# Second head's tiles in the input's even blocks, late gates by single column blocks, front inputs over attention's keys

## The chip, the cores and the metric

The kernel runs on one core of a Trainium2 chip. TensorE (PE in the profile) multiplies matrices into PSUM; VectorE (DVE), ScalarE (ACT) and GpSimd (POOL) work on SBUF and PSUM; SyncE (SP) issues the DMAs, from one queue and in order. The metric is the time of one execution on the device in microseconds. Before the change it is 1268.46 us, the median of three runs (1268.2 to 1274.1).

## The reference

One layer of a sequence mixer for a sequence of 2048 rows of 1024 numbers, in float32. The rows are normalised and multiplied by one wide input matrix, whose columns feed two groups of heads. Their outputs are gated, concatenated, projected and added to the input:

```python
h = rms_norm(x, norm_w[l])
proj = h @ w_in[l].astype(h.dtype)
(dn_q, dn_k, dn_v, dn_z, dn_beta, dn_decay,
 sw_q, sw_k, sw_v, sw_z) = jnp.split(proj, cuts, axis=-1)
dn = gated_deltanet_bidir(dn_q, dn_k, dn_v, dn_beta, dn_decay, ...)
dn = rms_norm(dn, dn_out_norm_w[l]).reshape(b, s, DN_WIDTH)
dn = dn * jax.nn.silu(dn_z.astype(jnp.float32))
sw = windowed_gqa_with_sinks(sw_q, sw_k, sw_v, swa_q_norm_w[l], swa_k_norm_w[l], swa_sinks[l])
sw = sw * jax.nn.silu(sw_z.astype(jnp.float32))
x = x + jnp.concatenate([dn, sw], axis=-1) @ w_out[l]
```

The first group ("dn") has four heads of 128. Its q, k and v pass through a short convolution over time; then each head runs a gated delta rule in both directions. In chunks, that rule needs the products of keys inside a chunk, the inverse of a unit triangular matrix for each chunk, and then a scan over the chunks that carries a 128 x 128 state. The second group ("sw") is attention in a window of 128 rows to either side, eight query heads on two key heads.

## The kernel before

The sequence is cut into 16 chunks of 128 rows, and for the input projection into four blocks of 512 (block 0 to 3). To reach float32 accuracy on the fast matmul type each operand is split into a high and a low part (`xhi`, `xlo`; `whi`, `wlo`), and a product is three matmuls: high by high, high by low, low by high. `proj_feat` (L189) makes one such unit: 8 row groups x 3 = 24 matmuls of 128 x 512 into one PSUM bank `pf_z` or `pf_c`.

`phase_a` (L71) works in two halves of two blocks each. It prepares the blocks (`xprep_rows`, `xprep`), projects attention's q, k, v (`seq_chunk`), and then runs attention chunk by chunk (`kv_chunk`, `q_chunk`, `attend`) with other projections between: the convolved dn columns (`conv_pair`) and the gates (`gate_pairs`, L210: tanh on ScalarE and one VectorE step make the SiLU of a gate, which is stored to DRAM in `zsw_d` and `zdn_d`). The split input lies in a pool `xp` with two buffers for each part, so blocks 0 and 2 share one and blocks 1 and 3 the other. Weights are loaded by `load_w` (L175) in pairs of 128-column groups: 256 KB pieces land in a staging tile `wst`, ScalarE copies the high part and VectorE subtracts to get the low one. Attention's keys and values lie in `k2` and `v2`.

The gates of the second half are the late gates: `phase_a` returns them as a list of functions (L414), and `phase_b` (L523) runs them behind the first head's front (L862 to L864). They use the pools `xp`, `wp` and a small output pool `zp`.

For each head h, `phase_b` has four steps; the first three of one head overlap with the scan of the head before:

- `pre_front(h)` (L610), the front: in four pieces of four chunks it loads `kq` and `vt` and the decays (`gm`), transposes, forms the key products `gh` (L667) and writes them, decayed, to the tiles `ma` (L676); it also writes `ks` and `vs` and stores part of `ma` to DRAM (`m_d`).
- `solve(h)` (L698) loads that back and inverts the 32 x 32 diagonal blocks in 31 serial steps on VectorE (`tm`, L714, and L718), then stores to `x_d`.
- `invert(h)` (L721) builds the 128 x 128 inverses from them, with matmuls `pi` (L745), in four parts.
- `scan(h)` (L771) has 16 steps for each direction; each forms `pk`, `py` and `po`. Each step's matmuls wait for the state of the step before.

The tiles `ma`, `ks` and `vs` of even heads lie in the pool `hd0`, those of odd heads in `hd1`; head 2 reuses the parts of `hd0` that scan 0 has left, head 3 those of `hd1`. `hd1` is allocated on the right side of SBUF after `wide.close()` (L871), where `xp`, `wp` and `zp` lay. So are `rp` (the scan's tiles), the scan's PSUM, `kx`, and `swp`, for the output product of the attention half (`sw_units`, matmuls `pcs`), which fills gaps between heads. `out_pair` (L928) makes the last product (`pcd`). `hd0`, `q1` (the front's inputs), `qa` and `qb` lie on the left, over the tiles of phase A that attention uses.

The order of the instructions on each engine comes from a planner, `set_order` (L1009). It builds a graph of all dependencies, buffers and pools, gives every instruction a cost, and schedules forward and backward in turn (L1308 to L1315); of the last passes it keeps the best and writes its order down for all five engines, the DMA queue on SyncE included. A pool laid over closed ones is planned behind all users of those. The first pass takes instructions by the length of the path behind them (`rank`).

Of the kernel before, what the change touches and what calls it, by code (L numbers as in the profile page):

```python
# [7 lines left out]
F32 = mybir.dt.float32  # L8
# [16 lines left out]
NDEC = 1  # L25
WSB = 7
# [9 lines left out]
def tile_hybrid(ctx, tc, t, out, dbg=None):  # L36
    nc = tc.nc
    V, A, G, T = nc.vector, nc.scalar, nc.gpsimd, nc.tensor
    dma = nc.sync.dma_start

    cp = ctx.enter_context(tc.tile_pool(reuse_waits="tile", name="cp", bufs=1))
    gp = ctx.enter_context(tc.tile_pool(reuse_waits="tile", name="gp", bufs=1))
    hp = ctx.enter_context(tc.tile_pool(reuse_waits="tile", name="hp", bufs=2))
    dp = ctx.enter_context(tc.tile_pool(reuse_waits="tile", name="dp", bufs=1, space=DRAM))

    def const(name, shape, src=None, dt=F32):
        a = cp.tile(shape, dt, tag=name, name=name)
# [12 lines left out]

    mix_dn = dp.tile([4, P, S], F32, tag="mix_dn", name="mix_dn")

    with ExitStack() as cb, ExitStack() as wide:
        with ExitStack() as ca:
            consts, late = phase_a(ca, wide, tc, t, ident, nw, bd, gp, mix_sw, kq_d, v_d, zdn_d, zsw_d, dp)
        phase_b(cb, wide, late, tc, t, ident, consts, hp, mix_dn, mix_sw, kq_d, v_d, zdn_d, zsw_d, dp, out)
    if dbg is not None:
        dbg(tc, locals())


def phase_a(ctx, wide, tc, t, ident, nw, bd, gp, mix_sw, kq_d, v_d, zdn_d, zsw_d, q_pool):  # L71
# [38 lines left out]
    def xprep_rows(b, then):  # L110
        xr = bp.tile([P, 1030], F32, tag="big", name=f"xr{b}_0")
        dma(xr[:, :D], t["x"][4 * b * P : (4 * b + 1) * P, :])
        for e in (b, b + 1):
            xhi[e] = xp.tile([P, KC, 512], F32R, tag="xhi", name=f"xhi{e}")
            xlo[e] = xp.tile([P, KC, 512], F32R, tag="xlo", name=f"xlo{e}")
# [37 lines left out]
    def xprep(b):  # L153
# [6 lines left out]
        if b not in xhi:  # L160
            xhi[b] = xp.tile([P, KC, 512], F32R, tag="xhi", name=f"xhi{b}")
            xlo[b] = xp.tile([P, KC, 512], F32R, tag="xlo", name=f"xlo{b}")
# [61 lines left out]

    def conv_pair(i0, half):
# [30 lines left out]
    k2 = ap.tile([P, 2, 2, 6 * P], F32R, tag="k2", name="k2")  # L256
    v2 = ap.tile([P, 6, 2, P], F32R, tag="v2", name="v2")
# [131 lines left out]
    for half in range(2):  # L389
# [22 lines left out]
        if half:  # L412
            fill = conv
            late = sw + [lambda zp, i=i: gate_pairs([(12 + i, zdn_d[i : i + 2])], half, None, zp) for i in (0, 2)]  # L414
# [108 lines left out]
def phase_b(ctx, wide, late, tc, t, ident, consts, hp, mix_dn, mix_sw, kq_d, v_d, zdn_d, zsw_d, dp, out):  # L523
# [66 lines left out]
    q1 = pool("q1")  # L590
    qa = pool("qa", stack=pre_stack)
# [10 lines left out]
    def ma_tile(h, p):  # L602
        tag = f"ma{FREED[p] if h > 1 else p}"
        return hd[h % 2].tile([P, 4, 4, P], F32, tag=tag, name=f"ma{h}_{p}", bufs=1)

    def kv_tile(kind, h, n, name):
        p, slot = ((0, n), (1, n), (2, n) if n < 2 else (0, n - 2), (0, 2 + n) if n < 2 else (1, n - 2))[h]
        return (hd[p] if p < 2 else kx).tile([P, 4, P], F32, tag=f"{kind}{slot}", name=name, bufs=1)

    def pre_front(h):  # L610
# [12 lines left out]
        for n, c4 in enumerate(FRONT):  # L623
            s4 = slice(4 * c4, 4 * c4 + 4)
            cs = slice(c4 * 512, (c4 + 1) * 512)
            kq = q1.tile([P, 2, 512], F32, tag="kq", name=f"kq{h}_{c4}", bufs=2)
            dma(kq, kq_d[h][:, :, cs])
            vt = q1.tile([P, 512], F32, tag="vt", name=f"vt{h}_{c4}", bufs=2)
            dma(vt, v_d[h][:, cs])
            gms = []  # L630
            for d in range(2):
                gm = q1.tile([P, 4, P], F32, tag="gm", name=f"dc{h}_{c4}_{d}", bufs=4)
# [253 lines left out]
    pair = [P, 2, 512]  # L886
# [10 lines left out]
    w = [spare(q1, pair, "kq", f"wod4_{x}", 2) for x in range(2)]  # L897
    wh.append([w[0][:, k] for k in range(2)])
    wl.append([w[1][:, k] for k in range(2)])
    w = [spare(q1, flat, "gm", f"wod5_{x}", 4) for x in range(4)]  # L900
    wh.append(w[:2])
    wl.append(w[2:])
    wh.append([spare(q1, flat, "vt", f"wod6_{k}", 2) for k in range(2)])
# [105 lines left out]
def set_order(tc):  # L1009
# [298 lines left out]
    now, best = plan([-r for r in rank], True), None  # L1308
# [71 lines left out]
```

## Time and profile before

| | us |
|---|---|
| median of 3 runs | 1268.46 |
| the profiled execution | 1270.95 |
| its span, first to last instruction | 1268.8 |
| TensorE busy | 1213.9 |
| VectorE busy | 918.6 |
| ScalarE busy | 716.8 |
| GpSimd busy | 562.6 |
| DMA moved | 205.34 MB, 162 GB/s mean |

Engines overlap, so the busy times don't add up. The record of a matmul covers its whole way through the array while the next one has already begun; two records that start 0.23 us apart last 0.4 us each, so the busy share of TensorE says where it has nothing to do rather than how much it does. Instructions bear the number of a line of the kernel and the names of the tiles: `pf_z<-xhi,wh_z` is a matmul of a gate. A float32 product that isn't split leaves two records for each matmul of the program.

### The profile page before, as it was taken

How to read it: one execution, taken by the hardware profiler on the slowest of the kernel's cores; microseconds unless marked ns; L12 is line 12 of the kernel's file. 1: busy time of each engine (PE TensorE's matmuls, PEld its weight loads, DVE VectorE, ACT ScalarE, POOL GpSimd, SP SyncE). 2: the span in 40 equal slices, each digit the busy share in tenths (PEclk: the TensorE clock that was granted, in tenths of full speed). 3: DMA queues.
4: the chain of work that ended last, by engine and by line, in shares of the span. 5: the costliest groups of instructions: out<-in, count | busy, mean ns of one | idle time of the engine just before them, and what ended most of it. 6: DMA issues, size and time to landing. Idle time of an engine off the chain costs nothing.

```text
span 1268.8 us, 22319 instructions
## 1 busy us (share of the span) xinstructions
PE 1213.9 (96%) x7018; PEld 1036.2 (82%) x7018; DVE 918.6 (72%) x2200; ACT 716.8 (56%) x2143; POOL 562.6 (44%) x941
## 2 busy tenths in 40 slices
PE   6999999999999999999999999899799899999998
PEld 5998888788879998778788787788588689889777
DVE  4412388999966479999996583679569869758765
ACT  6322254766644577776755424848566955686521
POOL 1430034667622288675321305513483373582442
PEclk9999999999999999999999999999899999999999
DMA  8442344332445434432128826976964885754786
GB/s 263 142 135 67 112 150 128 119 106 76 147 148 166 129 91 113 152 98 71 59 93 253 224 71 183 280 203 193 270 189 154 260 209 152 227 175 142 239 275 207
DMA packets 225765, 205.34 MB, mean 162 GB/s; under 512 B 48752, under 2 KB 175344, under 8 KB 225648
## 3 DMA queue, kind: packets, MB, share of 16 engines
q1 hardware_dynamic: 225648, 203.92, 53.0%
q8 instruction: 56, 0.92, 0.3%
q14 instruction: 61, 0.50, 0.1%
HBM read 138.79 MB, written 65.08 MB: 161 GB/s over the span
## 4 chain that ended last, share of the span: by engine, by line
PE 66%; DVE 11%; DMA 9%; ACT 8%; POOL 2%; issue 2%; SPq 1%; DVEq 0%; ACTq 0%; POOLq 0%
PE pf_c L194 4%; PE pf_c L195 4%; PE pf_c L196 4%; PE pf_z L194 4%; PE pf_z L195 4%; PE pf_z L196 4%; PE pi L745 3%; DVE acc L245 3%; PE pt L366 3%; DMA xr<-x 3%; PE pq_q L205 2%; PE pq_q L207 2%; PE pq_q L206 2%; PE pcd L958 2%; PE pcd L960 2%
## 5 line engine op out<-in xcount | busy, mean ns | idle before, releaser
L194 PE MATMUL pf_c<-xhi,wh_c 128*128 128x512 f32 x384 | 151.2, 404 | 0.7 <-DVE acc L245 0.4
L195 PE MATMUL pf_c<-xlo,wh_c 128*128 128x512 f32 x384 | 150.7, 402 | 0.0
L196 PE MATMUL pf_c<-xhi,wl_c 128*128 128x512 f32 x384 | 149.0, 401 | 0.0
L245 DVE SCALAR_TENSOR_TENSOR acc<-pf_c,cw,acc 128x512 f32<-128x512 f32 (+1 forms) x192 | 140.3, 742 | 11.1 <-ACT acc L241 9.1
L361 POOL TENSOR_SCALAR pr<-pr,st 128x384 f32<-128x384 f32 (+1 forms) x128 | 80.2, 644 | 71.8 <-DVE st L359 44.5
L194 PE MATMUL pf_z<-xhi,wh_z 128*128 128x512 f32 x256 | 86.7, 401 | 0.7 <-DVE zo L218 0.7
L352 ACT ACTIVATE pr<-pr,st 128x384 f32<-128x384 f32 (+1 forms) x128 | 76.1, 597 | 19.6 <-DVE st L348 19.2
L195 PE MATMUL pf_z<-xlo,wh_z 128*128 128x512 f32 x256 | 86.3, 399 | 0.0
L194 PEld LDWEIGHTS pf_c<-xhi,wh_c 128*128 128x128 f32 x384 | 72.1, 188 | 15.7 <-DVE acc L245 2.1
L196 PE MATMUL pf_z<-xhi,wl_z 128*128 128x512 f32 x256 | 84.8, 397 | 0.0
L195 PEld LDWEIGHTS pf_c<-xlo,wh_c 128*128 128x128 f32 x384 | 72.3, 188 | 12.9
L196 PEld LDWEIGHTS pf_c<-xhi,wl_c 128*128 128x128 f32 x384 | 71.8, 188 | 13.1
L348 DVE CUSTOM_DVE_ANT_0 pr<-s,mask,sink 128x384 f32<-128x384 f32 (+1 forms) x128 | 72.5, 593 | 12.5 <-PE s L347 8.1
L370 ACT ACTIVATE ph<-pt 128x512 fp32r<-128x512 f32 x92 | 52.9, 596 | 40.8 <-PE pt L366 38.9
L366 PE MATMUL pt<-ident,pr 128*128 128x128 f32 x368 | 67.3, 274 | 2.3 <-DVE q L330 1.1
L799 ACT ACTIVATE yk<-py,ck 128x128 f32<-128x128 f32 x120 | 43.6, 364 | 40.8 <-PE py L794 39.3
L371 DVE TENSOR_TENSOR pl<-pt,ph 128x512 fp32r<-128x512 f32 x92 | 61.6, 681 | 6.2 <-ACT ph L370 6.0
L572 PE MATMUL pcs<-wohs,mhs 128*128 128x512 f32 x128 | 57.3, 448 | 7.5 <-ACT mhs L566 4.6
L676 DVE SCALAR_TENSOR_TENSOR ma<-gh,bp,dc 128x256 f32<-128x256 f32 x128 | 54.7, 475 | 10.3 <-PE gh L667 7.6
L366 PEld LDWEIGHTS pt<-ident,pr 128*128 128x128 f32 x368 | 46.6, 140 | 18.3 <-POOL pr L361 3.2
L205 PE MATMUL pq_q<-wh_q,xhi 128*128 128x256 f32 x256 | 60.8, 287 | 0.3 <-ACT sgq L264 0.2
L206 PE MATMUL pq_q<-wh_q,xlo 128*128 128x256 f32 x256 | 60.6, 284 | 0.0
(276 smaller groups left out, 3792.0 us busy)
## 6 DMA issues: line engine op xcount, KB each, us to landing
kqc<-kq_d SPq DMA_DIRECT2D x120, 128.0 KB, 3.3
ws_c<-wt SPq DMA_DIRECT2D x48, 256.0 KB, 3.4
xr<-x SPq DMA_DIRECT2D x16, 512.0 KB, 6.4
ws_z<-wt SPq DMA_DIRECT2D x32, 256.0 KB, 3.9
kq<-kq_d SPq DMA_DIRECT2D x16, 512.0 KB, 5.1
m_d<-ma SPq DMA_DIRECT2D x32, 256.0 KB, 5.7
mxs<-mix_sw SPq DMA_DIRECT2D x32, 256.0 KB, 3.5
xrs<-x SPq DMA_DIRECT2D x32, 256.0 KB, 3.7
```

Of the source, the lines that this page charges most:

```text
L194: T.matmul(ps, hi[:, k, cs], xhi[b][:, k], start=(k == 0), stop=False)
L195: T.matmul(ps, hi[:, k, cs], xlo[b][:, k], start=False, stop=False)
L196: T.matmul(ps, lo[:, k, cs], xhi[b][:, k], start=False, stop=(k == KC - 1))
L205: T.matmul(ps[:, :n], xh, hi[:, k, :n], start=(k == 0), stop=False)
L206: T.matmul(ps[:, :n], xl, hi[:, k, :n], start=False, stop=False)
L245: V.scalar_tensor_tensor(av, ps[:, lo:], cw[:, i, k : k + 1], av, ALU.mult, ALU.add)
L348: V.tensor_tensor_reduce(pr[j][:, :n], ps[:, :n], mask[:, lo * P : hi * P], 1.0, sink[:, hh : hh + 1], ALU.add, ALU.min, accum_out=nm[:, j ...
L352: A.activation(pr[j][:, :n], pr[j][:, :n], AF.Exp, bias=nm[:, j : j + 1], scale=-1.0, accum_out=den[:, j : j + 1])
L361: G.tensor_scalar(pr[j][:, :n], pr[j][:, :n], den[:, j : j + 1], 1.0, ALU.mult, ALU.mult)
L366: T.transpose(pt[:, j], pr[j][:, (kb - lo) * P : (kb - lo + 1) * P], ident)
L371: V.tensor_tensor(pl, ptf, ph.bitcast(F32), ALU.subtract)
L572: T.matmul(ps, mh[:, k], wh[:, k], start=(k == 0), stop=False)
```

## The change

- **Split input.** The buffers of the even blocks move to a pool `xe` of their own and `k2` and `v2` to a pool `ae`. Both are allocated first on the right side and stay to the end. The odd blocks keep the pool `xp`, with one buffer.
- **Second head's tiles.** After block 2 the buffers of `xe` become `e1` and `e2`. They hold three of head 1's four `ma` tiles and two each of its `ks` and `vs`, and again head 3's. What is left of `hd1` (16 KB) moves to the left side and exists from the start.
- **Late gates.** One function `late_gates` replaces the list. It goes through 16 units (gate, block) in the order `LATE`, with block 2 done after twelve. It loads weights for one gate (128 columns) at a time into a pool `wz` with two buffers, in pieces of 128 KB, and loads gates 5 and 4 twice: ten loads of four pieces. `wp` closes with phase A.
- **Front's inputs.** `kq`, `vt` and three of four decay tiles are parts of two tiles laid over `k2` and `v2`; one decay tile stays in `q1`. The last product's weights that lay over these inputs move with them.
- **The planner's first pass** takes everything ahead of the first solve in program order, and the rest by rank as before.

The costs, the later passes and all arithmetic are as before.

```diff
+LATE = ((0, 2), (1, 2), (1, 3), (0, 3), (2, 2), (3, 2), (3, 3), (2, 3), (4, 2), (5, 2), (6, 2), (7, 2), (7, 3), (6, 3), (5, 3), (4, 3))
...
+        with tc.using_default_side("right"):
+            xe = cb.enter_context(tc.tile_pool(reuse_waits="tile", name="xe", bufs=1))
+            ae = cb.enter_context(tc.tile_pool(reuse_waits="tile", name="ae", bufs=1))
...
-        xp = wide.enter_context(tc.tile_pool(reuse_waits="tile", name="xp", bufs=2))
-        wp = wide.enter_context(tc.tile_pool(reuse_waits="tile", name="wp", bufs=2))
+        xp = xe, wide.enter_context(tc.tile_pool(reuse_waits="tile", name="xp", bufs=1))
+        wz = wide.enter_context(tc.tile_pool(reuse_waits="tile", name="wz", bufs=2))
+        wp = ctx.enter_context(tc.tile_pool(reuse_waits="tile", name="wp", bufs=2))
...
+    def late_gates(zp):
+        held = []
+        for i, b in LATE:
+            w = next((w for j, w in held if j == i), None)
+            if w is None:
+                w = [wz.tile([P, KC, P], F32R, tag=k, name=f"{k}{i}_{b}") for k in ("zhi", "zlo")]
+                col = (16 + i) // 2 if i < 4 else (8 + i) // 2
+                for kk in range(0, KC, 2):
+                    st = wz.tile([P, 2, P], F32, tag="zst", name=f"zs{i}_{b}_{kk}", bufs=2)
+                    dma(st, t["wt"][col][:, kk : kk + 2, i % 2 * P : (i % 2 + 1) * P])
+                    A.activation(w[0][:, kk : kk + 2], st, AF.Copy)
+                    V.tensor_tensor(w[1][:, kk : kk + 2], st, w[0][:, kk : kk + 2].bitcast(F32), ALU.subtract)
+                held = (held + [(i, w)])[-2:]
+            ps = proj_feat(w, 0, b, f"z{i}_{b}")
+            o = zp.tile([P, 512], F32, tag="big", name=f"zo{i}_{b}")
+            A.activation(o, ps, AF.Tanh, scale=0.5)
+            V.scalar_tensor_tensor(o, o, 1.0, ps, ALU.add, ALU.mult)
+            dma((zsw_d[i] if i < 4 else zdn_d[i - 4])[:, b * 512 : (b + 1) * 512], o)
...
-    k2 = ap.tile([P, 2, 2, 6 * P], F32R, tag="k2", name="k2")
-    v2 = ap.tile([P, 6, 2, P], F32R, tag="v2", name="v2")
+    k2 = ae.tile([P, 2, 2, 6 * P], F32R, tag="k2", name="k2")
+    v2 = ae.tile([P, 6, 2, P], F32R, tag="v2", name="v2")
...
+    q2, q3 = (ae.tile([P, n, 512], F32, tag=k, name=f"{k}_q") for k, n in (("k2", 6), ("v2", 3)))
+    hd.append(pool("hd1"))
...
+        slot = FREED[p] if h > 1 else p
+        if h % 2 and slot in mas:
+            return mas[slot]
...
-            kq = q1.tile([P, 2, 512], F32, tag="kq", name=f"kq{h}_{c4}", bufs=2)
+            kq = q2[:, 2 * (n % 2) : 2 * (n % 2) + 2]
             dma(kq, kq_d[h][:, :, cs])
-            vt = q1.tile([P, 512], F32, tag="vt", name=f"vt{h}_{c4}", bufs=2)
+            vt = q2[:, 4 + n % 2]
...
-        zp = pool("zp", 2, stack=wide)
+        zp = pool("zp", 4, stack=wide)
+    kvs = {}
     H = pre_front(0)
-    for f in late:
-        f(zp)
+    late(zp)
...
     invert(0, H)
+    e1, e2 = (xe.tile([P, 8, 4, P], F32, tag=k, name=f"{k}_h") for k in ("xhi", "xlo"))
+    mas = {1: e1[:, 0:4], 2: e1[:, 4:8], 0: e2[:, 4:8]}
+    kvs = {("ks", 0, 1): e2[:, 0], ("vs", 0, 1): e2[:, 1], ("ks", 1, 1): e2[:, 2], ("vs", 1, 1): e2[:, 3]}
     wide.close()
...
-        hd.append(pool("hd1"))
...
-    now, best = plan([-r for r in rank], True), None
+    stage = min(used[x][0] for x in used if x.startswith("L0_"))
+    now, best = plan([k - 1e9 if k < stage else -rank[k] for k in range(total)], True), None
```

More of the change, by code (lines that the diff above doesn't have):

```diff
@@ L113, in xprep_rows @@
         for e in (b, b + 1):
-            xhi[e] = xp.tile([P, KC, 512], F32R, tag="xhi", name=f"xhi{e}")
-            xlo[e] = xp.tile([P, KC, 512], F32R, tag="xlo", name=f"xlo{e}")
+            xhi[e] = xp[e % 2].tile([P, KC, 512], F32R, tag="xhi", name=f"xhi{e}")
+            xlo[e] = xp[e % 2].tile([P, KC, 512], F32R, tag="xlo", name=f"xlo{e}")
         nwb = bp.tile([P, 1030], F32, tag="big", name="nwb")[:, :D]
@@ L160, in xprep @@
         if b not in xhi:
-            xhi[b] = xp.tile([P, KC, 512], F32R, tag="xhi", name=f"xhi{b}")
-            xlo[b] = xp.tile([P, KC, 512], F32R, tag="xlo", name=f"xlo{b}")
+            xhi[b] = xp[b % 2].tile([P, KC, 512], F32R, tag="xhi", name=f"xhi{b}")
+            xlo[b] = xp[b % 2].tile([P, KC, 512], F32R, tag="xlo", name=f"xlo{b}")
         for k2 in range(4):
@@ L413, in phase_a @@
             fill = conv
-            late = sw + [lambda zp, i=i: gate_pairs([(12 + i, zdn_d[i : i + 2])], half, None, zp) for i in (0, 2)]
+            late = late_gates
         else:
@@ L520, in delta_setup, with phase_b @@
     return dmask, dnw, pw, beta, negc, ngc, egt, ekd, egc, gr_d, dec_d
-def phase_b(ctx, wide, late, tc, t, ident, consts, hp, mix_dn, mix_sw, kq_d, v_d, zdn_d, zsw_d, dp, out):
+def phase_b(ctx, wide, xe, ae, late, tc, t, ident, consts, hp, mix_dn, mix_sw, kq_d, v_d, zdn_d, zsw_d, dp, out):
     nc = tc.nc
@@ L885, in phase_b @@
         fill(1, bank(k % 2))
-    pair = [P, 2, 512]
     flat = [P, 512]
```

29 lines of the change are left out of this document (17 added, 12 removed).

## The prediction, made before the result was known

> **What bounds the kernel now.** I read the page's table of busy time first, then the stages, then single tiles inside the stages, and last the chain of waits.
>
> ```profile
> PE 1213.9 (96%) x7018; PEld 1036.2 (82%) x7018; DVE 918.6 (72%) x2200; ACT 716.8 (56%) x2143; POOL 562.6 (44%) x941
> ```
>
> TensorE is busy for 96% of the span, so a change that removes no matmul can only take back what TensorE idles, plus what it loses to a lower granted clock. The next view cuts the span at the events of the program: the end of the first part, the end of the late gates, and the starts and ends of the four heads' scans. Its columns are the stretch, its length, the busy time and count of each engine, the granted clock, the DMA share and GB/s.
>
> ```profile
> 0.00:32.00 32.00, 20.15 (x122) 18.33 (x123) 14.92 (x26) 19.73 (x40) 6.34 (x18) 0.95 0.81 264
> ...
> 0.00:674.00 674.00, 656.99 (x3657) 558.94 (x3658) 495.95 (x1065) 377.65 (x898) 302.91 (x479) 0.99 0.39 123
> 674.00:777.00 103.00, 102.11 (x467) 82.77 (x466) 61.14 (x147) 38.03 (x129) 21.72 (x38) 1.00 0.59 172
> 777.00:893.00 116.00, 105.28 (x712) 93.44 (x711) 88.21 (x266) 86.85 (x350) 48.66 (x87) 0.99 0.80 229
> 893.00:925.00 32.00, 22.89 (x110) 17.78 (x109) 14.54 (x41) 15.26 (x66) 18.07 (x42) 0.89 0.94 268
> 925.00:1006.00 81.00, 77.24 (x545) 69.23 (x544) 69.09 (x210) 59.31 (x231) 40.19 (x65) 0.98 0.63 183
> 1006.00:1030.00 24.00, 21.64 (x121) 16.68 (x120) 16.36 (x44) 16.91 (x69) 17.07 (x44) 1.00 0.96 280
> 1030.00:1108.00 78.00, 75.23 (x539) 68.13 (x538) 64.34 (x194) 43.85 (x147) 38.24 (x82) 1.00 0.65 184
> 1108.00:1183.00 75.00, 73.32 (x537) 66.03 (x535) 51.54 (x142) 53.03 (x187) 39.18 (x69) 1.00 0.57 170
> 1183.00:1268.00 85.00, 79.18 (x346) 63.20 (x345) 57.40 (x94) 25.87 (x71) 36.58 (x40) 1.00 0.74 244
> ```
>
> Idle TensorE is length less busy time. Of the 17.0 us before 674, 11.9 are the start-up in the first 32 us. From 674 to 777 it is 0.9, from 777 to 893 10.7, from 893 to 925 9.1, from 925 to 1006 3.8, and from 1006 to 1030 2.4. In 893:925 the granted clock is also only 0.89, which is 32 x 0.11 = 3.5 us more. So the stretch between scan 0 and scan 1 is the worst of the program. At the same time the stage of the late gates uses VectorE for 61 of 103 us and ScalarE for 38. The windows of single tiles tell why. They give, for `gh` (the key products of a front), `tm` (the solve) and `py` (the scan), the busy times inside each stretch.
>
> ```profile
> 676.00:716.00 40.00, 8.21 (x32) 5.76 (x32) 11.68 (x28) 1.00 0.82 248
> ...
> 778.00:818.00 40.00, 8.40 (x32) 5.39 (x32) 12.29 (x30) 0.96 0.90 261
> ...
> 866.00:911.00 45.00, 10.04 (x32) 5.70 (x32) 13.30 (x31) 0.92 0.83 237
> ```
> ```profile
> 731.00:764.00 33.00, 21.20 (x62) 1.00 0.23 72
> ...
> 839.00:896.00 57.00, 21.89 (x61) 1.00 0.67 198
> ...
> 936.00:1006.00 70.00, 26.86 (x61) 0.98 0.59 179
> ```
> ```profile
> 792.00:893.00 101.00, 12.70 (x64) 10.57 (x64) 16.98 (x61) 0.98 0.80 229
> 893.00:925.00 32.00, 0.00 (x0) 0.10 (x1) 0.26 (x1) 0.89 0.94 268
> 925.00:1007.00 82.00, 12.96 (x64) 10.39 (x64) 16.92 (x62) 0.98 0.64 184
> ```
>
> A head takes 32 products `gh`, 62 solve steps and 64 `py` (two records for each fp32 product). Front 0 has its products at 676 to 716 and solve 0 follows at 731 to 764, beside the late gates. Front 1 has them at 778 to 818, right behind the last gate; solve 1 runs at 839 to 896, spread out by the scan's VectorE work (21.9 us of work in 57, where solve 0 had 21.2 in 33). Then comes the inversion, and scan 1 starts at 925 though scan 0 was over at 893. That hole is head 1 being late, and head 1 is late because its tiles lie where the input blocks and the gates' weights lie until the last gate.
>
> **The change part by part.**
>
> *Head 1's tiles in the even block's space.* Front 1 now waits for block 2's last reader, the twelfth of sixteen gate units, and not for the last. A unit is 24 matmuls, which are spaced by 0.23 us in the timeline (start, length), and the gates' window counts 384 of them:
>
> ```profile
> 674.39 0.40 PE L194 MATMUL pf_z<-xhi,wh_z 128*128 128x512 f32 x1
> 674.63 0.40 PE L195 MATMUL pf_z<-xlo,wh_z 128*128 128x512 f32 x1
> 674.86 0.39 PE L196 MATMUL pf_z<-xhi,wl_z 128*128 128x512 f32 x1
> ```
> ```profile
> 674.00:778.00 104.00, 94.47 (x384) 71.24 (x384) 9.51 (x15) 8.96 (x16) 1.00 0.58 171
> ```
>
> So the gates are 384 x 0.232 = 89 us of TensorE, and what else ran in 674:777 is 102 - 89 = 13 us. Twelve units are 67 us; with the 13 of front 0 the block is free at about 754, with a few us for weights that come late (below) 757. Front 1 then starts 21 us earlier than 778. With the lags of the present run kept, solve 1 starts at 818 and scan 1 at 904. The hole shrinks from 32 to 11 us, and of its 9.1 + 3.5 = 12.6 us the same share, 21/32, returns: -8 (bounds: 0, if head 1 gains nothing; -12.6). What is late next: front 2 needs the tiles that scan 0 frees, at 866 to 911, and that is not moved by an earlier front 1; so scan 2's start at 1030 gains only what solve 2 (936) has waited for VectorE. From the 2.4 us idle there I take -1 (0 to -2.4).
>
> The clock: the 0.89 stands in the row where TensorE idles 28% of the time, and rows with under 5% idle have 0.98 to 1.00. The Trainium skill (TensorE: Matmul & The Clock Gate, What's actually happening) has the array's clock halved after about 3.4 us of idleness. The trace agrees in direction (0.89 at the hole); by that rule a hole that is filled without such pauses returns all 3.5 us of clock, where I took 21/32 of them, so the sum would be 1 us lower.
>
> *Front's inputs over attention's keys.* The first loads of `kq` and `vt` may start when the last scores are done, and now start behind attention's last store:
>
> ```profile
> 652.50 0.37 PE L347 MATMUL s<-k,q 128*128 128x256 f32 x1
> ...
> 668.15 0.32 SPq L385 DMA_DIRECT2D mix_sw<-ot  x1
> ...
> 669.35 0.60 SPq L627 DMA_DIRECT2D kq<-kq_d  x1
> ```
>
> Room for 16 us, but front 0's results still lie over attention's other tiles and its PSUM banks, so at most the 8 us from 668 to the first product at 676 are won. The gain passes on to solve 0 and inversion 0, whose matmuls then lie among the gates and not, as now, behind them, where scan 0 starts at 792 and waits for them. I take half of the 10.7 us that 777:893 idles: -5 (0 to -10.7), half because the gates' 89 us remain and whatever is pulled ahead of their end pushes it back.
>
> *Late gates by single column blocks.* Weights are loaded for one gate (128 columns), two are held, and the order needs ten loads of four pieces, 40 in place of 16. The conversions: 16 x (0.631 + 0.722) us now; 40 x (0.378 + 0.556) then, by the nearest rows of 256 elements (groups by line: busy us, mean ns | idle before). Behind them stand the page's rows of DMA issues, with KB and us to landing.
>
> ```profile
> L185 ACT ACTIVATE wh_z<-ws_z 128x512 fp32r<-128x512 f32 x32 | 19.9, 631 | 38.1 <-DMA ws_z<-wt 17.8 <-PE pf_z L195 10.6 <-PE pq_q L206 8.5
> L186 DVE TENSOR_TENSOR wl_z<-ws_z,wh_z 128x512 fp32r<-128x512 f32 x32 | 23.0, 722 | 18.6 <-ACT wh_z L185 18.4
> L264 ACT ACTIVATE sgq<-pq_q 128x256 f32<-128x256 f32 x32 | 11.1, 378 | 18.9 <-PE pq_q L207 12.1 <-DMA kv<-kv_d 5.2 <-ACT wh_c L185 0.9
> L953 DVE TENSOR_TENSOR mld<-mxd,mhd 128x256 fp32r<-128x256 f32 x16 | 8.8, 556 | 0.4 <-ACT mhd L952 0.4
> ```
> ```profile
> kqc<-kq_d SPq DMA_DIRECT2D x120, 128.0 KB, 3.3
> ...
> ws_z<-wt SPq DMA_DIRECT2D x32, 256.0 KB, 3.9
> ```
>
> That is +5 us of ScalarE and +10.7 of VectorE, in a stage where they have 65 and 42 us free: 0, covered by the gates' matmuls. If that cover goes, the VectorE part falls on the solve's serial steps. The 24 added issues stand on SyncE's queue, in order, ahead of `kq`, `m_d` and `xc`; each waits for a staging tile, so a late subtraction holds up the loads behind it. The chain of one load is 3.3 + 0.38 + 0.56 = 4.2 us by these rows; with two staging tiles a gate's four pieces are two such rounds, 8.5 us against the 5.6 us of its unit. Units 5, 6 and 9 to 12 each bring a new gate: (8.5 - 5.6) x 5 = 15 us. Where a gate's slot comes free only as its first unit should start (units 5, 9 and 15, since slots go round) the second half lands a round later, 4.2 + 0.9 us against the 2.8 us that the first half lasts: 2.3 x 3 = 7 us. Together 22 us of holes, if TensorE had nothing else. Beside it lie the 13 us of front 0, as much of front 1, and inversion 0. So 0 to +22; I take +3, near the covered end, since 26 us of cover stand against 22.
>
> The price of the 128 KB piece is latency more than size: 3.3 us, against 3.9 for twice the bytes. The Trainium skill (DMA: Bandwidth & Descriptors, Specifications) gives line rate from 512 B on, which is just the run of a 128-column row, and about 0.6 us to the first byte. By its 435 GB/s a piece would take an estimated 0.9 us, a gate 3.7, and there would be no holes: the sum would be 3 us lower. The row decides.
>
> *The planner's first order* keeps program order up to the first solve. That can move work in the first 674 us, which idles 17.0 - 11.9 = 5.1 us past its start. I take 0, between -5 and +5. *Pools and final weights in other places*: same counts of buffers, no added instruction, 0; the final weights are made long after the last front.
>
> The sum: -8 - 1 - 5 + 3 = -11. The profiled execution took 1270.95 us with a span of 1268.8, and lies 2.5 above the median 1268.46; taken off the median this is 1257.
>
> **The rivals.**
> (a) *All the idle time returns.* Head 1 has its inversion ready when scan 0 ends, and inversion 0 is done before scan 0: -12.6 - 10.7 - 2.4 = -25.7, and 1243. For it: VectorE's and ScalarE's free time among the gates. Against it: DMA share 0.94 and 0.96 in both holes, which also load the output products' inputs.
> (b) *Nothing moves.* TensorE stays with the gates to the end because their 89 us must run somewhere ahead of scan 0; whatever front 1 wins pushes the last gates back by the same time, and scan 2 waits on front 2 as now. Then 1268, give or take 3. For it: 96% busy, and 0.9 us idle in 674:777.
> (c) *The gates become bound by their weights*, and the kernel is slower. The place is units 5 to 15, the price the 22 us of holes less what covers them. It decides when the planner leaves front 0 ahead of unit 5 (its products were done at 716, eight units after the start) and front 1 behind unit 12: then only the last 4 units have cover, some 11 us of holes stay, block 2 is freed 11 us later and the 8 us of head 1 are mostly gone. 1268 + 11 = 1279.
>
> **How the numbers follow.** Chances: the forecast 0.40, (a) 0.18, (b) 0.17, (c) 0.25. Half a percent, 6.3 us, is about what a measurement of this kernel can tell from no change. Forecast and (a) are faster: 0.58; (b) is the same, 0.17; (c) slower, 0.25. The forecast alone spans 1248 to 1262. The range runs from the sum of all lower bounds, 1268.5 - 12.6 - 10.7 - 2.4 - 5 = 1238, to (c) with 2 us of a worse order in the first part, 1281.
>
> **What the profile afterwards would show.** Right: `gh` of the second head starts at 750 to 760, before the last `zo`; `py` has no hole of 30 us near 893:925, or the clock there is 0.95 or more; the first `kq` load is issued before 660. The gates' stage keeps TensorE idle under 3 us. Wrong: gaps before the gates' matmuls released by the new weight copies (ScalarE or VectorE), a front 1 that still starts behind the last gate, a hole between scan 1 and scan 2 that has grown by what the first one lost, or a first part that ends more than 5 us away from 674.

## The result, and the profile after

The changed kernel takes 1277.29 us (median of 14 runs, 1271.36 to 1282.37) where the kernel before takes 1269.65 (14 runs too). The ratio is 1.0054, with a 95% interval from 1.0038 to 1.0071: 7 us slower, where 11 us faster was forecast.

The profiled execution took 1282.01 us with a span of 1280.2. It lies 4.7 us above its median, and the one of before 1.3 above 1269.65, so the two traces differ by 11.4 us where the medians differ by 7.6. The stages of the kernel after, cut at the same events as before (columns: stretch, length, busy time and count of PE, PEld, DVE, ACT, POOL, then granted clock, DMA share, GB/s):

```profile
0.00:667.00 667.00, 649.21 (x3635) 553.79 (x3636) 497.78 (x1054) 375.44 (x887) 297.27 (x474) 1.00 0.38 123
667.00:682.00 15.00, 14.27 (x68) 10.66 (x67) 12.19 (x26) 8.73 (x19) 7.49 (x12) 1.00 0.62 204
682.00:795.00 113.00, 104.03 (x484) 82.74 (x483) 66.90 (x188) 55.42 (x218) 24.96 (x38) 0.98 0.66 189
795.00:805.00 10.00, 8.98 (x63) 8.41 (x62) 4.98 (x15) 8.64 (x36) 7.01 (x16) 0.89 0.77 228
805.00:894.00 89.00, 84.45 (x585) 75.88 (x585) 73.16 (x217) 63.93 (x240) 37.82 (x66) 1.00 0.76 228
894.00:921.00 27.00, 19.28 (x110) 15.83 (x108) 14.42 (x45) 15.34 (x66) 13.94 (x31) 0.94 0.91 262
921.00:1006.00 85.00, 78.59 (x551) 70.87 (x551) 70.00 (x210) 58.90 (x229) 43.98 (x76) 0.98 0.65 183
1006.00:1036.00 30.00, 23.67 (x116) 18.56 (x115) 14.98 (x43) 17.64 (x72) 16.27 (x41) 0.83 0.79 238
1036.00:1110.00 74.00, 70.61 (x509) 64.64 (x509) 61.99 (x182) 42.78 (x143) 34.01 (x74) 1.00 0.63 182
1110.00:1189.00 79.00, 77.07 (x570) 70.31 (x568) 54.32 (x156) 54.05 (x190) 43.73 (x78) 1.00 0.57 172
1189.00:1280.00 91.00, 82.97 (x346) 65.48 (x345) 56.39 (x94) 25.79 (x72) 36.70 (x41) 0.95 0.71 229
```

TensorE's idle time is again length less busy time. The first part starts the late gates at 667 instead of 674. The gates' stage (667 to 795) lasts 128 us instead of 103 and idles 9.7 us where it idled 0.9. The stretch of scan 0 (795 to 894) idles 5.6 us in place of 10.7, and scan 0 ends at 894, 1 us after before: most of the 11.4 us arise behind it. The hole to scan 1 is 27 us with 7.7 idle, where it was 32 us with 9.1. The hole to scan 2 has grown: 30 us, 6.3 idle at a clock of 0.83, where it was 24 us with 2.4 idle at 1.00. The end, from 1189, is 6 us longer at a clock of 0.95 and idles 8.0 us in place of 5.8.

The windows of the key products `gh` (fronts 0 and 1) and of the scan's `py`:

```profile
685.00:718.00 33.00, 8.37 (x32) 5.72 (x32) 11.83 (x28) 1.00 0.75 227
718.00:807.00 89.00, 8.70 (x32) 5.92 (x32) 14.04 (x33) 0.96 0.64 179
```
```profile
805.00:895.00 90.00, 12.93 (x64) 10.32 (x64) 16.88 (x62) 1.00 0.76 230
895.00:921.00 26.00, 0.00 (x0) 0.00 (x0) 0.00 (x0) 0.93 0.90 257
921.00:1006.00 85.00, 13.22 (x64) 10.57 (x64) 16.87 (x61) 0.98 0.65 183
1006.00:1036.00 30.00, 0.00 (x0) 0.00 (x0) 0.33 (x1) 0.83 0.79 238
```

Front 0 starts at 685, not at 668 and not even at 676, because attention itself ends later. The last product with its values, in the timeline of before and of after:

```profile
666.04 0.40 PE L374 MATMUL po<-pl,v 128*128 128x512 f32 x1
```
```profile
679.82 0.39 PE L398 MATMUL po<-pl,v 128*128 128x512 f32 x1
```

Front 1 does begin among the gates. Its first four products run at 729, into PSUM; block 2's tiles are first written at 762, and the other products run from 771 on and end at 807, 11 us earlier than before and not 21. The waits of the changed kernel from 667 to 805 (who waited for whom, us in total, times, longest), the rows of the new weight tiles (durations in ns, least, median, most), and pieces of the chain that ended last in this stretch (start, length; the profile calls the tile of `kq` and `vt` `k_q`):

```profile
ACT zhi L240 <- DMA zs<-wt: 32.3, 19, 6.0
DVE zlo L241 <- ACT zhi L240: 19.5, 12, 4.3
...
PE tr L682 <- DMA k_q<-kq_d: 4.2, 2, 3.9
...
PE pf_z L199 <- DVE zo L246: 2.2, 1, 2.2
...
PE pf_z L201 <- DVE zlo L241: 0.9, 2, 0.5
```
```profile
L240 ACT ACTIVATE zhi<-zs x32: 400/418/432, 694.9 to 783.7; 128x256 fp32r<-128x256 f32 x32
L241 DVE TENSOR_TENSOR zlo<-zs,zhi x32: 393/418/990, 695.4 to 784.2; 128x256 fp32r<-128x256 f32 x32
...
DMA to landing us min/median/max: 2.4/3.6/6.6
```
```profile
775.82 6.63 DMA zs<-wt
782.47 0.42 ACT zhi L240
782.88 0.49 ACT ks L685
783.42 0.67 PE tr L682 x4
...
785.30 8.07 DMA k_q<-kq_d
```

ScalarE sits before the new copies for 32 us, until a piece of weights has landed. The copies go on to 784, and the last gate ends at 795. TensorE itself waits for the new weights for only 0.9 us; it waits longer for work that stood behind them. The 2.2 us are a wait, up to 732.5, for a gate's output `zo`: its tanh ran on ScalarE at 731, behind copies that had waited for landings until 727.7 and 728.8. The 3.9 us are front 1's last load of `kq`. The chain shows that it went out only when a landing, a copy and the front's next steps were through; it took 8 us, and the transposes and the gates' last matmuls stood still behind it. The loads of weights are late in their turn: SyncE holds them back until VectorE has freed a staging tile, while VectorE works through solve 0 (`X` and `tm`):

```profile
SPq L239 <- DVE X L753: 11.4, 7, 2.2
```

### The profile page after: what moved, and what is told of

Same layout as the page of the kernel before. It is cut to its first block, busy times and chain, and to the rows that moved or that the text cites. A ratio compares the mean times of both kernels' runs of the same rounds, so it can differ in the third digit from the quotient of the medians.

```text
span 1280.2 us, 22373 instructions
## 1 busy us (share of the span) xinstructions
PE 1213.1 (95%) x7018; PEld 1037.2 (81%) x7018; DVE 927.1 (72%) x2224; ACT 726.7 (57%) x2167; POOL 563.2 (44%) x941
## 5 line engine op out<-in xcount | busy, mean ns | idle before, releaser
L199 PE MATMUL pf_c<-xhi,wh_c 128*128 128x512 f32 x384 | 155.5, 405 | 1.1 <-DVE acc L269 1.0
L200 PE MATMUL pf_c<-xlo,wh_c 128*128 128x512 f32 x384 | 154.9, 403 | 0.0
L201 PE MATMUL pf_c<-xhi,wl_c 128*128 128x512 f32 x384 | 154.4, 402 | 0.0
L199 PEld LDWEIGHTS pf_c<-xhi,wh_c 128*128 128x128 f32 x384 | 72.5, 189 | 13.2 <-DVE acc L269 1.5
L201 PEld LDWEIGHTS pf_c<-xhi,wl_c 128*128 128x128 f32 x384 | 72.3, 188 | 12.4
L211 PE MATMUL pq_q<-wh_q,xlo 128*128 128x256 f32 x256 | 72.1, 282 | 0.0
L212 PE MATMUL pq_q<-wl_q,xhi 128*128 128x256 f32 x256 | 71.9, 281 | 0.0
L210 PE MATMUL pq_q<-wh_q,xhi 128*128 128x256 f32 x256 | 71.4, 280 | 0.0
L692 POOL TENSOR_TENSOR nk<-ssk,pw 128x4 f32<-128x4 f32 x16 | 16.4, 1026 | 109.6 <-DVE ssk L691 109.6
L191 DVE TENSOR_TENSOR wl_c<-ws_c,wh_c 128x512 fp32r<-128x512 f32 x48 | 40.3, 842 | 22.2 <-ACT wh_c L190 16.8
L597 PE MATMUL pcs<-wohs,mls 128*128 128x512 f32 x128 | 55.6, 435 | 0.4 <-DVE mls L591 0.4
```

The lines of the kernel that those rows point to most:

```text
L199: T.matmul(ps, hi[:, k, cs], xhi[b][:, k], start=(k == 0), stop=False)
L200: T.matmul(ps, hi[:, k, cs], xlo[b][:, k], start=False, stop=False)
L201: T.matmul(ps, lo[:, k, cs], xhi[b][:, k], start=False, stop=(k == KC - 1))
L211: T.matmul(ps[:, :n], xl, hi[:, k, :n], start=False, stop=False)
L212: T.matmul(ps[:, :n], xh, lo[:, k, :n], start=False, stop=(k == KC - 1))
L597: T.matmul(ps, ml[:, k], wh[:, k], start=False, stop=False)
```

## The experiments

Three theories stood against each other. W: the gates are bound by loading their weights. P: the particular order that the planner found is to blame. H: full DMA queues between the scans eat the gain. C came up on the way: the time runs through the even heads, since front 2 waits for scan 0. All ratios are to the kernel before, on the same chip.

**The changed kernel again**, as the reference for its variants.

> The changed kernel as it is, beside its variants on the same chip. Both theories expect what the 14 runs gave: about 1277 us, 0.5% above the kernel before, with the late gates ending near 795 in the trace.

1278.04 us, ratio 1.0069 (1.0048 to 1.0091). The slowdown is there again.

**Most of the weights' loads left out.**

```diff
-            w = next((w for j, w in held if j == i), None)
+            w = next((w for j, w in held if j % 2 == i % 2), None)
```

> Left out: the weights of late gates 2 to 7; those units use the weights of gates 0 and 1, so eight of ten loads and their 32 copies and subtractions are gone. Theory W (the late gates are bound by loading their weights one gate at a time): the gates end 12 to 18 us earlier than 795 and the whole becomes 8 to 14 us faster than the changed kernel, 1263 to 1269. Theory P (the new order that the planner found, and the late end of attention, cost the time; weights only fill it): under 4 us, 1273 to 1277.

1272.43 us, ratio 1.0003 (0.9985 to 1.0021). The gates end at 776, about as W has it, but of 8 to 14 us expected only 6 show; the time lies between the two theories' ranges. The order of the instructions is another one here, as in every run below that doesn't say otherwise.

**Eight loads in place of ten.**

```diff
-LATE = (..., (4, 2), (5, 2), (6, 2), (7, 2), (7, 3), (6, 3), (5, 3), (4, 3))
+LATE = (..., (4, 2), (5, 2), (5, 3), (4, 3), (6, 2), (7, 2), (7, 3), (6, 3))
```

> Only the order of the units: eight loads in place of ten, none twice, with block 2 free after fourteen units in place of twelve. Theory W: two loads of 8.5 us are gone, 3 to 6 us faster than the changed kernel, 1271 to 1274. If instead the early release of block 2 is worth more than the loads, front 1 starts 11 us later and the time is 1280 or more. Theory P: no difference, 1275 to 1280.

1268.96 us, ratio 0.9990 (0.9971 to 1.0008): 9 us faster than the changed kernel beside it, more than W's 3 to 6. The gates end at 777, as early as with two loads.

**The planner's first pass by rank again** (the last part of the change undone).

```diff
-    now, best = plan([k - 1e9 if k < stage else -rank[k] for k in range(total)], True), None
+    now, best = plan([-r for r in rank], True), None
```

> The changed kernel with the planner's first pass by rank alone, as before. If the new first pass did the harm (theory P in its narrow form), this is faster than the changed kernel, 1265 to 1272. If it was needed for the new layout, it is slower, 1285 or more.

1297.72 us, ratio 1.0221 (1.0199 to 1.0242). The new first pass doesn't do the harm; without it the new layout costs 20 us more. It is also a first sign of how much one order differs from another.

**Block 3 first**, with eight loads: block 2 is read until the last gate.

```diff
+LATE = ((0, 3), (1, 3), (1, 2), (0, 2), (2, 3), (3, 3), ..., (6, 3), (7, 3), (7, 2), (6, 2))
```

> The eight-load order with blocks 2 and 3 exchanged, so that block 2 is read until the last gate unit and front 1 can write its tiles only then. Same loads, same work. If an early front 1 is worth what was forecast, this is 6 to 10 us slower than the eight-load order with block 2 first (1269), 1275 to 1279. If the gain of an early front 1 is lost again before scan 1 (theory H: the holes between the scans are set by full DMA queues, not by when front 1 starts), it is within 3 us of it, 1266 to 1272.

1266.70 us, ratio 0.9970 (0.9951 to 0.9989). Not slower but, if anything, faster. The early release of block 2, which is half of the change's idea, is worth nothing that shows in this pair; under another plan (below) the comparison turns round. The windows of `gh` (front 1) and `py` (scan 1), first with block 2 first, then with block 3 first:

```profile
758.00:800.00 42.00, 9.68 (x32) 5.99 (x32) 12.87 (x31) 0.92 0.79 211
```
```profile
917.00:1001.00 84.00, 12.93 (x64) 10.17 (x64) 17.19 (x62) 1.00 0.68 193
```
```profile
766.00:805.00 39.00, 8.91 (x32) 5.31 (x30) 11.86 (x28) 0.91 0.82 226
```
```profile
912.00:998.00 86.00, 12.59 (x64) 10.40 (x64) 17.35 (x62) 1.00 0.67 194
```

With block 2 first, front 1 is over at 799, 18 us earlier than in the kernel before; scan 1 starts at 918, 7 us earlier. With block 3 first, front 1 is over 5 us later and scan 1 starts 5 us sooner. So an early front doesn't carry through to its scan by the same amount. Against the kernel before, the 18 us are lost along the way with block 2 first: the last store of front 1's `ma` goes out at 809 instead of 822, the load of `L` for the solve at 820 instead of 829, and the solve's first step comes at 831 instead of 839. These stores and loads stand in SyncE's queue.

**Four staging tiles.**

```diff
-                    st = wz.tile([P, 2, P], F32, tag="zst", name=f"zs{i}_{b}_{kk}", bufs=2)
+                    st = wz.tile([P, 2, P], F32, tag="zst", name=f"zs{i}_{b}_{kk}", bufs=4)
```

> The changed kernel, ten loads, with four staging tiles in place of two. If the two-tile round of landing, copy and subtraction holds the gates (theory W by its staging), the gates end 5 to 10 us earlier and the time is 1268 to 1273. If it is the weight slots that come free late, or the two loads too many, it stays at 1275 to 1279.

1272.40 us, ratio 1.0009 (0.9991 to 1.0026), 5 us faster than the changed kernel's 1277 to 1278; the gates end at 779. This is for W, but the planner had made another order as well.

**Loads of x left out of the attention half's output product**, with eight loads.

```diff
-            dma(xr, t["x"][c * P : (c + 1) * P, ns])
...
-            V.tensor_tensor(xr, xr, ps, ALU.add)
+            V.tensor_copy(xr, ps)
```

> The eight-load order with the loads of x left out of the attention half's output product: 32 loads of 256 KB less, and the sum's input is missing in the output. Theory H: the holes at 777 to 807, 891 to 918 and 1000 to 1030 have DMA shares of 0.84 to 0.99; with 8 of some 110 MB behind 777 gone they shorten, and the time falls by 4 to 10 us, to 1259 to 1265. If the holes are latency of solve and inversion alone, under 2 us.

1270.78 us, ratio 0.9988 (0.9973 to 1.0002), level with the 0.9990 of the same kernel with these loads. The three holes, first with the loads, then without:

```profile
777.00:807.00 30.00, 20.98 (x107) 17.10 (x106) 15.39 (x37) 19.25 (x69) 21.20 (x47) 0.83 0.94 266
891.00:918.00 27.00, 20.47 (x113) 17.07 (x113) 14.72 (x42) 15.80 (x67) 15.49 (x38) 0.87 0.96 273
1000.00:1030.00 30.00, 24.57 (x122) 19.05 (x121) 17.85 (x46) 16.91 (x68) 17.87 (x42) 0.89 0.84 226
```
```profile
777.00:811.00 34.00, 27.55 (x174) 22.94 (x173) 20.14 (x46) 25.59 (x95) 25.12 (x62) 1.00 0.93 276
888.00:913.00 25.00, 18.65 (x100) 15.73 (x99) 13.16 (x36) 12.81 (x53) 16.36 (x41) 0.86 0.92 257
1000.00:1024.00 24.00, 20.87 (x124) 17.72 (x125) 15.98 (x40) 18.74 (x75) 18.86 (x43) 1.00 0.81 234
```

Idle falls from 9.0, 6.5 and 5.4 us to 6.5, 6.4 and 3.1, and the clock rises in two of the three, but the time doesn't follow. The DMA shares hardly fall either. Theory H, that fewer bytes shorten the kernel, gets no support, but with one order on each side a gain of some us could be hidden; what a high share delays other than by bytes, such as the order of the queue, was not tried.

**One part of the change alone: front's inputs over attention's keys, in the kernel before.**

```diff
-            kq = q1.tile([P, 2, 512], F32, tag="kq", name=f"kq{h}_{c4}", bufs=2)
+            kq = q2[:, 2 * (n % 2) : 2 * (n % 2) + 2]
```

(with `k2`, `v2`, `vt` and three decay tiles moved as in the change)

> The kernel before with one part of the change: the front's inputs over attention's keys and values. The forecast gave this part -5 us with the first loads of a front at 653 instead of 669: 1263 to 1267. If nothing is gained because the front's results still wait for attention's last tiles, 1267 to 1274; a worse plan of the whole order would show as more than 1276.

1281.80 us, ratio 1.0075 (1.0049 to 1.0101): about 10 us slower, which the expectation had named as a worse plan. The first `kq` load goes out at 662 instead of 669, but attention's last product is at 676 instead of 666 and front 0's first at 680 instead of 676. That attention ends late isn't the luck of one plan: in all 17 traces of kernels with these tiles moved, attention's last product lies between 676 and 712; in the three plans of the kernel before (two of them below) it lies at 666. Why the planner does that stays open.

**Half of a solve left out**, for head 1 and for head 2, with eight loads.

```diff
-        for c in range(31):
+        for c in range(0, 31, 1 + (h == 1)):
```

> The eight-load order; every second step of head 1's solve is left out (16 of 31 steps), so head 1's inverse is wrong. Head 1's solve ends some 20 to 30 us earlier, well beyond what an early front 1 gave. Theory C (the time runs through the even heads: attention's end, front 0, scan 0, front 2 over scan 0's tiles, solve 2, scan 2): scan 1 starts earlier, waits arise in front of scan 2 instead, and the time is within 3 us of 1269. The forecast's theory (the hole between scan 0 and scan 1 costs the time): 7 to 13 us faster, 1256 to 1262.

> The same cut in head 2's solve. Theory C: scan 2 starts 15 to 25 us earlier and the time falls by 6 to 15 us, to 1254 to 1263. If TensorE's work is all that counts, or both heads weigh alike, it changes as much as the cut in head 1 does.

Head 1's cut gives 1261.64 us, ratio 0.9927 (0.9901 to 0.9952); head 2's 1270.88, ratio 0.9997 (0.9978 to 1.0016). This is against C, and nearer to the forecast's theory that head 1's solve is on the path. For each of the two, the window of `py` where the scan of the cut head begins:

```profile
895.00:900.00 5.00, 0.45 (x2) 0.30 (x2) 0.00 (x0) 1.00 0.84 218
```
```profile
1006.00:1020.00 14.00, 0.00 (x0) 0.00 (x0) 0.30 (x1) 1.00 0.81 234
1020.00:1040.00 20.00, 2.49 (x12) 1.81 (x12) 2.90 (x11) 1.00 0.83 232
```

In the first, scan 1 starts at 899 instead of 918. In the second, scan 2 starts at 1021 instead of 1030, but in that order attention ended at 689 and scan 0 at 898, 7 us later than with eight loads uncut. So each cut moves its own scan, and the order moves the whole by as much. With one order for each this pair doesn't settle which head counts.

**The same programs under other plans.** The changed kernel with 30 planner passes in place of 12:

```diff
-    for i in range(12):
+    for i in range(30):
```

> The changed kernel with 30 planner passes in place of 12: the same instructions, loads and tiles in another order. It says what a change of order alone is worth. If the ten loads hold the gates whatever the order (theory W), 1273 to 1279; if the loss was the bad luck of one plan (theory P), 1264 to 1272.

1272.63 us, ratio 1.0007 (0.9992 to 1.0023): 5 us less, by the order of the same instructions alone. The kernel with block 3 first, under the same edit:

> The eight-load order with block 3 first, the best kernel so far (1266.7), with 30 planner passes. Order alone: 1262 to 1270.

1270.76 us, ratio 0.9994 (0.9974 to 1.0014): 4 us more, and 0.6% above block 2 first under the same 30 passes (0.9935, below). So which block should go first stays open, and no single pair of runs above tells a cause of that size from an order. Two kinds of experiments do. One keeps the order to the instruction: four staging tiles, while the planner counts two.

```diff
+            need += -(-m.max_size_bytes // P // grain) * grain * (2 if tag == "zst" else m.bufs)
+            home[f"{tag}_{name}_{p.id}"] = (name, 2 if tag == "zst" else m.bufs)
```

> The changed kernel with four staging tiles while the planner still counts two, so every engine's order is that of the changed kernel to the instruction. Theory W by staging: the gates end 5 to 15 us earlier than 795 and the time is 1268 to 1273. If the earlier four-tile run gained by its other order only, 1275 to 1280.

1274.36 us, ratio 1.0024 (1.0005 to 1.0042), where the same order with two tiles has 1.0054 (1.0038 to 1.0071): about 3 us of the 7 are the wait for a free staging tile. The two intervals still overlap a little, and the time lies between what W and its opposite expected. It is the only experiment here on the weights with the order held. Its waits and its gates' stage:

```profile
ACT zhi L240 <- DMA zs<-wt: 27.8, 12, 6.6
```
```profile
682.00:793.00 111.00, 103.95 (x491) 84.08 (x491) 68.72 (x190) 54.92 (x220) 24.92 (x38) 0.98 0.69 190
```

The gates still end at 793: SyncE's 11.4 us before `X` are 2.6 here, but ScalarE waits for landings nearly as long. The other kind runs three plans for each of the three programs:

```diff
-LAG = {"PE": 205, "DVE": 140, "Activation": 160, "Pool": 120, "SP": 2400}
+LAG = {"PE": 210, "DVE": 140, "Activation": 160, "Pool": 120, "SP": 2400}
```

> The changed kernel, one planner cost (TensorE's lag) 210 in place of 205: the same instructions in another order. If the changed program is slower whatever the plan, 1273 to 1281; if 1277 was one bad plan, 1266 to 1273.

> The kernel before under the same change of one planner cost. If plans of one program differ by some 5 us, this is 1265 to 1277; if the kernel before holds its time against plans, 1268 to 1272.

> The eight-load order under the same change of one planner cost. If eight loads are what counts, it stays under the ten-load kernel with the same cost by 4 us or more, 1266 to 1272; if plans decide, it may be anywhere from 1266 to 1280.

> The kernel before with 30 planner passes, a third plan of it. If the plan that was measured as the kernel before is a good one among worse, 1272 to 1282; if 210 was one bad plan, 1266 to 1272.

> The eight-load order with 30 planner passes. If eight loads keep the gates from the weights in any plan, 1264 to 1270, under each plan of the ten-load kernel.

| ratio to the kernel before (95%) | plan as it was | lag 210 | 30 passes | mean |
|---|---|---|---|---|
| kernel before | 1 | 1.0093 (1.0061 to 1.0124) | 1.0034 (1.0015 to 1.0053) | 1.0042 |
| changed, ten loads | 1.0054 (1.0038 to 1.0071) | 1.0053 (1.0033 to 1.0072) | 1.0007 (0.9992 to 1.0023) | 1.0038 |
| changed, eight loads | 0.9990 (0.9971 to 1.0008) | 0.9957 (0.9940 to 0.9974) | 0.9935 (0.9915 to 0.9955) | 0.9961 |

In microseconds: before 1269.65, 1280.37, 1270.68; changed 1277.29, 1276.91, 1272.63; eight loads 1268.96, 1265.38, 1259.11. They come from several chips, and only the ratios compare: on the chip of 1270.68 and 1259.11 the kernel before with its own plan took 1267.41. The last is faster than both kernels.

Two readings follow. Down a column, ten loads cost 0.64%, 0.96% and 0.72% against eight: 8, 12 and 9 us. A column shares the planner's setting and not the order, so these are three draws and no pinned pairs; but every ten-load plan lies above every eight-load plan. The eight-load order also frees block 2 two units later, so the number of loads isn't all that differs. Along the first row, the kernel before is slower by 0.9% and 0.3% under the other two plans; its own plan was the best of the three. The change as drawn is slower than before under one plan of three, and faster by 0.4% and 0.3% under the other two, at the edge of their intervals; by the means of three plans the two are level. With three plans each, no rate for other plans can be given.

The traces say where the ten loads lose. Plan by plan, the gates end at 795, 787 and 792 with ten loads and at 777, 782 and 780 with eight, and scan 0 ends at 894, 892 and 892 against 891, 888 and 882. So 3, 5 and 10 us are lost by the end of scan 0. The spans of these traces differ by 13, 14 and 17 us; the rest arises behind scan 0, and no run shows why.

The gates' stage of the fastest kernel, eight loads with 30 passes, in stages and in its wait for weights and its copies:

```profile
664.00:682.00 18.00, 17.89 (x88) 14.04 (x88) 14.47 (x30) 10.02 (x23) 5.21 (x12) 1.00 0.66 225
682.00:781.00 99.00, 96.12 (x466) 78.99 (x465) 65.41 (x175) 49.74 (x203) 23.88 (x35) 1.00 0.66 186
781.00:791.00 10.00, 9.70 (x68) 8.12 (x67) 6.83 (x16) 9.80 (x41) 8.01 (x20) 1.00 1.02 284
791.00:883.00 92.00, 86.84 (x592) 78.10 (x590) 74.94 (x229) 65.29 (x254) 37.95 (x67) 0.98 0.77 225
883.00:909.00 26.00, 19.97 (x100) 15.63 (x101) 12.58 (x35) 13.55 (x54) 16.31 (x39) 0.93 1.00 308
```
```profile
ACT zhi L240 <- DMA zs<-wt: 20.6, 12, 5.1
```
```profile
L240 ACT ACTIVATE zhi<-zs x24: 402/418/437, 691.1 to 757.5; 128x256 fp32r<-128x256 f32 x24
```

The copies are over at 758 instead of 784 and ScalarE waits 21 us for them instead of 32. TensorE idles 2.9 us from 682 to 781, where the changed kernel idles 9.0 from 682 to 795. Scan 0 ends at 882 and not at 894. The hole behind it is still there, 26 us at a DMA share of 1.00.

## Why the prediction was wrong

*The weights of the late gates* are the term that was mis-sized. The working had 0 to +22 us and took +3, "near the covered end", because 26 us of other TensorE work stood beside 22 us of holes. Measured by ten loads against eight it is 8 to 12 us, in three plans. The wait also lies elsewhere than the working had it. It had TensorE wait for the copies of each gate; measured, that is 0.9 us. What broke the cover is that it hung on the same queues. Half of the cover, front 1, shares the SyncE queue and ScalarE with the loads and came late itself: its last `kq` load took 8 us. The gates' own outputs stood behind the copies on ScalarE, which is the 2.2 us up to 732.5. And there was little other work where the new weights were wanted: from 731 to 759, 96 of TensorE's 104 matmuls are the gates' own (L199 to L201: 33, 32 and 31), and 2.5 us idle, 1.5 of them the end of the wait for `zo`. From 775 to 795, before and during that load of `kq`, it idles 5.0 us:

```profile
731.00:759.00 28.00, 25.48 (x104) 19.39 (x105) 20.50 (x55) 10.15 (x31) 1.11 (x2) 0.94 0.56 156
```
```profile
775.00:795.00 20.00, 15.00 (x75) 11.75 (x75) 9.38 (x27) 10.24 (x45) 9.77 (x24) 0.97 0.89 236
```

These are most of the stage's 9.7. Rival (c) named the weights as the cause, the stage and 1279 us, and the measured 1277 is nearest to it. That the numbers meet is in part luck: its 11 us of holes were to lengthen the program directly, while here scan 0 ends only 1 us late and the loss arises behind it; and block 2 is free at 762, 5 us after the forecast's 757 and not 11. The steps' own prices held up: a landing took 3.6 us against the 3.3 used, a copy 418 ns against 378 and a subtraction 418 ns against 556. The working has a slip that changes nothing here: it lists six units that bring a new gate and multiplies by five, so its 22 us should be 24.

*The planner's order* was bounded by 5 us to either side, and only for the first 674 us. The kernel before alone spans 10 us over three plans, and orders differ after scan 0 as much as before it. Behind 894 the changed kernel's profiled span idles 33.8 us (the last six stages), that of before 25.5 behind 893: about 8 us of the 11.4 by which the traces differ arose there, where the change moves tiles but adds and removes no instruction. That the kernel before stood on a good plan was not in any rival. By the three plans' means, eight loads stand 0.8% or 10 us below the kernel before, where under the old plan they stand 1 us below it: of that difference 5 us are the good plan of the kernel before, and 4 us that eight loads have their worst of three there. That this 10 is close to the forecast 11 is luck and doesn't confirm its gains, which didn't come the way it had them.

*Head 1's tiles* (-8): front 1 was to start at 757 and scan 1 at 904. In the changed kernel `gh` was over at 807 and scan 1 began at 921; with eight loads at 799 and 918. The first link, an earlier front, is right when the weights don't hold it. The second, that the lags behind it stay as they are, failed: 18 us earlier at the front's end are 7 us at the scan, after 13 us at the last store of `ma` and 8 us at the solve's first step. That a hole filled before scan 1 does shorten the kernel is supported by half a solve left out for head 1: scan 1 19 us earlier, the time 0.6% below the uncut eight loads, in one order. Whether the early release of block 2 helps stays open: against block 3 first it loses 0.2% under one plan and gains 0.6% under another.

*What is late next*: the place was named rightly and the sign was not. The hole before scan 2, which was to lose 1 us, grew from 24 to 30 us, and scan 1's gain of 4 us was gone at its end (1006 in both). The prediction had listed such a growth among the signs of being wrong, as it had a first part that ends over 5 us away from 674 (667).

*Front's inputs over attention's keys* (-5) went the wrong way. The first load was to be issued at 653 and went out at 667, since attention's last scores moved to 667. Front 0 began at 685 instead of 668. The step that failed is that the scores would stay at 652 when the tiles move: they end late in every kernel with moved tiles. What that costs is open: in the changed kernels the gates start earlier in their place, and the eight-load ones are faster than before all the same. The part alone, in the kernel before, cost 10 us in one order; its sign over several orders wasn't measured.

*The clock*: that holes bring the clock down is right. The hole before scan 2 has 0.83, that before scan 1 0.94. The prediction didn't foresee that new holes elsewhere (0.89 at 795 to 805, 0.95 in the last stage) would cost clock of their own, nor that one short hole is enough (last section).

## What to carry to other kernels

When the order of a kernel is found by a heuristic, the change and its side effect on the order are measured together. Run the old and the new program under two or three other plans, or pin the order, before a difference of half a percent is put down to the edit. An early release of a buffer has to be weighed against the second load of weights that it asks for: count the loads of each weight along the new order, and check the copy chain's length against the work of its own unit, not against cover that waits in the same queue or behind the same copies on ScalarE. An earlier producer shortens the time only as far as every later lag stays constant; take the gain from where the consumer's own inputs end, not from where the producer starts.

## What the hardware showed that was not expected

A hole costs clock beyond its own length, and not the same each time. In the changed kernel the 2.2 us hole up to 732.5 is followed by 3.4 us at half the clock, in which matmuls start 0.43 us apart instead of 0.23:

```profile
732.40:735.80 3.40, 3.29 (x8) 2.51 (x9) 2.57 (x5) 1.97 (x9) 0.00 (x0) 0.50 0.85 160
```

The hole before scan 2 has 6.3 us idle and a clock of 0.83 in this trace. In the trace of the changed kernel again, with the same order on every engine, the same hole idles 7.0 us and has 0.94:

```profile
1010.00:1038.00 28.00, 20.99 (x116) 17.14 (x116) 15.69 (x43) 17.31 (x72) 15.99 (x42) 0.94 0.85 254
```

The 14 runs of this program spread by 0.9% (1271.36 to 1282.37), and the mean granted clock went with the time. The two runs with 0.992 took 1271.4 and 1273.5 us and the one with 0.993 took 1275.4; the three with 0.984 or 0.985 took 1278.3, 1281.6 and 1281.8. The five runs of the changed kernel again don't keep to that: 1276.8 us with 0.985 and 1278.0 with 0.992. The instructions and their order are the same in all, so how much clock the holes cost differs from run to run. The Trainium skill (TensorE: Matmul & The Clock Gate, What's actually happening) describes a gate that judges activity in a window of 3.4 us which runs free of the program. The trace agrees with the length: the half clock above lasts 3.4 us. That the spread comes from where the holes fall in that window is an inference from the page, and no run here shows it.
